# A hybrid diffusion block on one core: both token parts of a product in one 512-column matmul, each in its half of a PSUM bank, and down tiles between all up groups

## The chip, the core and the metric

The kernel runs on 1 core of one Trainium2 chip. The metric is the device time of one execution in microseconds, the lower the better. Engines are called TensorE (PE in rows; its weight loads PEld), VectorE (DVE), ScalarE (ACT), GpSimd (POOL) and SyncE (SP, which issues most loads).

## What is computed

One layer (`DEPTH = 1`) over 512 tokens of width 2048: a conditioned norm, a chunked gating MLP, a second norm, and a gated FFN with a width-3 convolution along the tokens. Only the FFN is touched by the change:

```
def conv_ffn(h, w_up, conv_w, conv_b, w_down):
    z = dwconv(h @ w_up, conv_w, conv_b, FFN_CONV // 2)
    g, v = jnp.split(z, 2, axis=-1)
    return (jax.nn.silu(g) * v) @ w_down
...
h_lat = h_lat + m_l[:, :, 5] * conv_ffn(n_l, ffn_w_up[i], ffn_conv_w[i], ffn_conv_b[i], ffn_w_down[i])
return rmsnorm(h_lat, final_g)
```

`w_up` is 2048 x 11264 (5632 gate and 5632 value columns), `w_down` 5632 x 2048.

## The kernel before

**Number format.** Every factor is split into a high part, rounded to the type that TensorE multiplies, and a low part, what is left (`split`, L71: the high one on ScalarE, L72, the low one on VectorE, L73). A product is three matmuls, `mm3` (L66): high weights x high tokens, high x low, low x high. Weights are the stationary operand and are loaded anew for each matmul.

**The FFN in chunks.** The 5632 columns are 11 chunks (`fc`) of 512. Chunk 0 runs plainly (`f0_comp`, `f1_comp`, in halves of 256 tokens). Chunks 1 to 10 save one multiplication in eight: for a pair of 128-row tiles of the tokens and a pair of 128-column tiles of the weights, the 2 x 2 x 2 products over the two token halves are replaced by **7 products** of sums and differences, each 128 x 128 weights by 256 tokens. `t_pair` (L667) makes the sums of tokens once; `s_prep` (L773) loads the weights of two pairs, forms their 4 sums on VectorE (L778 to L780) and splits both: a tile of 768 columns (plain weights) and one of 1024 (sums).

**Units.** All work is a list of units. An *up group* (`up_group`, L964) makes 256 of the gate columns (`vpart` 0) or value columns (`vpart` 1) of a chunk: 4 units, each `s_comp` with two pairs. The 7 products are summed over all 8 pairs in PSUM, two products in the halves of one bank, 4 banks. `s_evac` (L792) then forms the four results from the seven sums with one ScalarE copy and 4 VectorE additions, in the tile `z`, and `conv_evac` (L693) does the convolution, the SiLU, and for a value group the product with the gate and its split. A *down* unit (`d_comp`, L866) is 24 matmuls of 512 columns; two of them fill 4 banks, and `d_evac` (L844) scales each bank into a tile `a` (pool `part`, 3 buffers) and GpSimd adds that to `hD` in device memory by a DMA.

**What sets the order.** The loop over units (L1022) calls a unit's `comp`, then the `prep` of the unit two further on (`LOOK = 2`), and between them takes `deferred` work with `pop`. `s_evac`, `conv_evac` and `d_evac` are deferred. From there a scheduler sets each engine's queue, which then runs in order. Of the tiles, `wpool` has 4 high and 4 low buffers (an up unit takes two of each, a down unit one), `raw` 6 buffers for loads and sums, `ps` 8 PSUM banks. Per chunk the order of units is (L973): up, 4 down, up, 4 down, up, up; in the last chunk up, 2 down, up, 2 down, up, up, 4 down.

```
                for out, (sh, sl), q, mov, new in (
                        (d[:, L], (h3, l3), 0, lo(X1), True),
...
                    mm3(out, sh[:, k, q, :], sl[:, k, q, :], *mov, first and new, last, True)
```

Of the kernel before, what the change touches and what calls it, by code (L numbers as in the profile page):

```python
# [12 lines left out]
P = 128  # L13
# [23 lines left out]
def build(tc, ctx, x, xT, cvec, adaT, ada_b, norm_g, w_in, g_v, w_sT, b_s, w_out,  # L37
# [588 lines left out]
    x1, x2, x3, x4, b12 = [{} for _ in range(5)]  # L626
# [4 lines left out]
    tmade = [0]  # L631
# [5 lines left out]
    def pair_t(dst, p):  # L637
        if p not in dst:
            dst[p] = blk_t(F32R), blk_t(F32R)
        return dst[p]  # L640
# [3 lines left out]
    def n_tile(th, d):  # L644
# [3 lines left out]
        def f():  # L648
# [6 lines left out]
            if th == 0:  # L655
                h, l = pair_t(x1, p)
                split(h[:, half(j)], l[:, half(j)], t)
            elif j == 0:
                b12[p] = blk_t(F32R)
                split(b12[p][:, L], b12[p][:, R], t)  # L660
            else:
                h, l = pair_t(x2, p)
                split(h[:, L], l[:, L], t)
# [3 lines left out]
    def t_pair(p):  # L667
        def f():
# [6 lines left out]
            h, l = pair_t(x2, p)  # L675
# [38 lines left out]
    def half_tok(th, k):  # L714
        p, j = k // 2, k % 2
        if th == 0:
            return [x[:, half(j)] for x in x1[p]]
        if j == 0:
            return b12[p][:, L], b12[p][:, R]
        return [x[:, L] for x in x2[p]]  # L720

# [10 lines left out]
    def f_mm(th, k2, w):  # L732
        h, l = w
        for i in range(4):
            for a in range(2):
# [4 lines left out]
                mm3(state["fp"][i][:, half(th)], h[:, cs], l[:, cs], *half_tok(th, k),  # L740
# [19 lines left out]
    def f1_comp(k2):  # L760
        def f(w):
# [30 lines left out]
    def s_evac(cp, acc):  # L792
        a, b, c, d = acc

        def f():
            z = spat.tile([P, D], F32, tag="s", name="z")

            def at(i, n=1):
                return z[:, i * HT:(i + n) * HT]
            two = lambda x: x.rearrange("p (n t) -> p n t", n=2)  # L800
            dup = lambda x: x.unsqueeze(1).to_broadcast([P, 2, HT])
# [5 lines left out]
            state["z", cp] = z  # L807
        return f

    def s_comp(fc, i2, vpart, u):  # L810
        cp = vpart * (FF // 256) + fc * 2 + i2

        def f(w):
            (h3, l3), (h4, l4) = w
            while tmade[0] < min(2 * u + 2, NP):
                pop()
            if u == 0:
                state["sp7"] = [bank() for _ in range(4)]
            a, b, c, d = state["sp7"]
            for k in range(2):  # L820
                p = 2 * u + k
                X1, X2, X3 = x1[p], x2[p], x3[p]
                X4 = x4[p][:, L], x4[p][:, R]
                lo = lambda x: [y[:, L] for y in x]
                hi = lambda x: [y[:, R] for y in x]
                first, last = p == 0, p == NP - 1
                for out, (sh, sl), q, mov, new in (
                        (d[:, L], (h3, l3), 0, lo(X1), True),
# [37 lines left out]
    def d_comp(fc, q):  # L866
        def f(w):
# [4 lines left out]
            for i in range(4):  # L872
# [4 lines left out]
                if q % 2:  # L877
                    deferred.append(d_evac(fc, q // 2 * 4 + i, state["dp"][i]))
# [220 lines left out]
```

## Time and profile before

| | us |
|---|---|
| median of 3 runs | 2536.16 (2535.04 to 2540.63) |
| the profiled execution | 2533.04 |
| its span, first to last instruction | 2531.3 |
| TensorE busy (matmuls) | 2488.6, 98% |
| TensorE weight loads | 2223.9, 88% |
| VectorE busy | 1759.8, 70% |
| ScalarE busy | 1100.1, 43% |
| mean granted TensorE clock | 0.997 of full speed |

The busy share of TensorE counts pipelined matmuls, so it doesn't tell how near each matmul is to its shortest spacing; that is read from the starts of neighbouring matmuls. VectorE's next operation starts some 0.08 us before the end of the one ahead, so what an operation costs in a full queue is also read from start to start. The FFN's chunks 1 to 10 run from about 1195 to 2475 us.

### The profile page before, as it was taken

Reading aid. Unit: us, or ns where it says so; the run is one execution under the profiler, and the core shown is the slowest. Engines: PE = TensorE matmul, PEld = TensorE weight load, DVE = VectorE, ACT = ScalarE, POOL = GpSimd, SP = SyncE. Lnnn points to the kernel's source line nnn. Section 1 sums busy time; section 2 is a strip of 40 time slices with the busy share of each in tenths; the row PEclk is TensorE's granted clock in tenths of the full one; section 3 lists DMA queues with packets and bytes.
Section 4 is the critical chain, followed back from the end, with each engine's and each line's share of the span. In section 5 each row is a group of like instructions: output and inputs, shape, how many; then the busy total and the mean of one; then the engine's idle time right before and its main releaser. Section 6 shows DMA issues by size and latency. Waiting matters only on the chain.

```text
span 2531.3 us, 37809 instructions
## 1 busy us (share of the span) xinstructions
PE 2488.6 (98%) x14888; PEld 2223.9 (88%) x14888; DVE 1759.8 (70%) x2877; ACT 1100.1 (43%) x1595; POOL 149.4 (6%) x182
## 2 busy tenths in 40 slices
PE   7999999999999999999999999999999999999998
PEld 5888888878888888899999999999999999999998
DVE  6895577567676437469658686767677777767775
ACT  7422234333334224347445454545444444444454
POOL 0000000000000000000010101111111111111011
PEclk9999999999999999999999999999999999999999
DMA  7885555555555446524364655555555556565573
GB/s 274 293 309 188 190 185 187 171 173 186 182 187 183 157 157 210 199 90 136 94 141 135 141 133 134 139 135 140 128 147 129 148 120 157 118 150 117 142 193 107
DMA packets 166042, 411.69 MB, mean 163 GB/s; under 512 B 15460, under 2 KB 25828, under 8 KB 165864
## 3 DMA queue, kind: packets, MB, share of 16 engines
q1 hardware_dynamic: 139432, 361.04, 44.5%
q0 software_dynamic: 24320, 46.15, 11.5%
q8 instruction: 116, 1.90, 0.3%
q10 hardware_dynamic: 2112, 2.10, 0.2%
q14 instruction: 62, 0.51, 0.1%
HBM read 358.89 MB, written 50.33 MB: 162 GB/s over the span
## 4 chain that ended last, share of the span: by engine, by line
PE 83%; DMA 7%; DVE 7%; issue 2%; ACT 1%; SPq 0%; DVEq 0%; ACTq 0%
PE p L62 83%; DMA r<-in_adaT 6%; DVE r L131 2%; DVE wl L73 2%; DMA r<-in_w_in 1%; ACT wh L72 1%; DVE b L367 0%; DVE b L73 0%; DVE b L468 0%; DVE sp L450 0%; DVE b L471 0%; DVE b L362 0%; DVE r L930 0%; ACT b L270 0%; ACT b L72 0%
## 5 line engine op out<-in xcount | busy, mean ns | idle before, releaser
L62 PE MATMUL p<-b,wh 128*128 128x256 f32 (+1 forms) x8256 | 1905.4, 325 | 0.1
L62 PEld LDWEIGHTS p<-b,wh 128*128 128x128 f32 x8256 | 1388.9, 190 | 126.2 <-ACT wh L72 0.3
L62 PE MATMUL p<-b,wl 128*128 128x256 f32 (+1 forms) x4128 | 1340.0, 325 | 2.9 <-DVE wl L73 2.8
L72 ACT ACTIVATE wh<-r 128x1024 fp32r<-128x1024 f32 (+2 forms) x457 | 438.2, 969 | 970.2 <-PE p L62 792.3
L62 PEld LDWEIGHTS p<-b,wl 128*128 128x128 f32 x4128 | 784.6, 190 | 68.0 <-DVE wl L73 3.7
L73 DVE TENSOR_TENSOR wl<-r,wh 128x1024 fp32r<-128x1024 f32 (+2 forms) x457 | 505.0, 1110 | 207.7 <-ACT wh L72 207.0
L131 DVE SCALAR_TENSOR_TENSOR r<-r,cb 128x1024 f32<-128x1024 f32 x192 | 233.4, 1222 | 263.3 <-DMA r<-in_adaT 262.4
L62 PE MATMUL p<-wh,b 128*128 128x512 f32 x992 | 310.4, 391 | 0.8 <-ACT wh L72 0.8
L848 POOL DMA_DIRECT2D hD<-a x160 | 139.7, 907 | 2294.8 <-ACT a L847 2293.8
L73 DVE TENSOR_TENSOR wl<-s,wh 128x1024 fp32r<-128x1024 f32 x160 | 195.6, 1222 | 106.6 <-ACT wh L72 106.6
L62 PEld LDWEIGHTS p<-wh,b 128*128 128x128 f32 x992 | 186.2, 188 | 40.0 <-ACT wh L72 1.9
L62 PE MATMUL p<-wl,b 128*128 128x512 f32 x496 | 193.8, 391 | 3.1 <-DVE wl L73 3.1
L778 DVE TENSOR_TENSOR s<-r 128x512 f32<-128x512 f32 x160 | 110.0, 688 | 100.5 <-DMA r<-in_w_up 99.5
L72 ACT ACTIVATE wh<-s 128x1024 fp32r<-128x1024 f32 x160 | 167.6, 1048 | 19.5 <-PE p L62 19.4
L847 ACT ACTIVATE a<-p,m 128x512 f32<-128x512 f32 x160 | 109.0, 686 | 127.6 <-DMA hD<-a 79.8
L62 PEld LDWEIGHTS p<-wl,b 128*128 128x128 f32 x496 | 93.2, 188 | 24.4 <-DVE wl L73 5.6
L62 PE MATMUL p<-b 128*128 128x256 f32 (+1 forms) x624 | 85.0, 297 | 5.3 <-ACT b L72 5.3
L62 PEld LDWEIGHTS p<-b 128*128 128x128 f32 x624 | 79.5, 194 | 9.1 <-ACT b L72 6.6
L780 DVE TENSOR_TENSOR s<-s,r 128x256 f32<-128x256 f32 x160 | 67.7, 423 | 3.8
L779 DVE TENSOR_TENSOR s<-s,r 128x256 f32<-128x256 f32 x160 | 67.6, 422 | 3.8
L73 DVE TENSOR_TENSOR b<-b 128x512 fp32r<-128x512 f32 (+3 forms) x117 | 62.4, 561 | 5.2 <-ACT b L72 4.8
L72 ACT ACTIVATE b<-b 128x512 fp32r<-128x512 f32 (+3 forms) x117 | 55.8, 518 | 1.3 <-DVE b L672 1.1
(109 smaller groups left out, 1150.7 us busy)
## 6 DMA issues: line engine op xcount, KB each, us to landing
r<-in_adaT SPq DMA_DIRECT2D x192, 512.0 KB, 4.5
r<-in_w_up SPq DMA_DIRECT2D x184, 512.0 KB, 3.7
r<-in_w_in SPq DMA_DIRECT2D x121, 512.0 KB, 4.1
r<-in_w_down SPq DMA_DIRECT2D x88, 512.0 KB, 4.9
hD<-a POOLq DMA_DIRECT2D x160, 256.0 KB, 5.2
r<-in_w_out SPq DMA_DIRECT2D x64, 512.0 KB, 4.7
b<-in_x SPq DMA_DIRECT2D x16, 256.0 KB, 5.4
b<-in_xT SPq DMA_DIRECT2D x16, 256.0 KB, 6.5
```

The source lines that it names most:

```text
L62: nc.tensor.matmul(out, lhsT, rhs, start=first, stop=last, skip_group_check=shared)
L72: nc.scalar.activation(hi, src, AF.Copy)
L73: nc.vector.tensor_sub(lo, src, hi.bitcast(F32))
L131: nc.vector.scalar_tensor_tensor(r[b], r[b], 1.0, state["cb"][b], op0=ALU.mult, op1=ALU.mult, accum_out=m2[:, b, j:j + 1])
L778: nc.vector.tensor_add(s[:, :, 0:2, :], r[:, :, 0:1, :].to_broadcast([P, 2, 2, P]), r[:, :, 1:4:2, :])
L779: nc.vector.tensor_add(s[:, :, 2, :], s[:, :, 1, :], r[:, :, 1, :])
L780: nc.vector.tensor_add(s[:, :, 3, :], s[:, :, 2, :], r[:, :, 2, :])
L847: nc.scalar.activation(t, p, AF.Copy, scale=m[:, 5 * ND + d:5 * ND + d + 1])
L848: nc.gpsimd.dma_start(out=hD[d * P:(d + 1) * P, :], in_=t, accum_op=ALU.add)
```

## The change

Each operand of tokens is now one tile, `tok[name, pair]`, with its high part in the left 256 columns and its low part in the right ones (`tok_split`; the names are B11 to B22, N1, N2, T3, T4). A product is `mm3w`: the high weights times the whole tile, 512 columns, and the low weights times the left half, 256 columns. The sum of a product therefore fills a whole bank, high part left and low part right, and an up group has 7 banks. `s_evac` adds the two halves as well. It and `d_evac` are called at once and not deferred; `conv_evac` stays deferred, and `s_evac` first takes all that read the one `z` tile (`zlive`). Behind the first value chunk (`f1_comp`) the four banks are copied to `z`, and the convolution reads them there. Two down units stand behind each up group; in the last chunk behind the first two groups, and four at the end, as before.

```diff
+    def mm3w(bank, sh, sl, w, first, last):
+        n = w.shape[-1] // 2
+        mm(bank, sh, w, first, False, True)
+        mm(bank[:, :n], sl, w[:, :n], False, last, True)
...
+    def tok_split(name, p, src):
+        t = tok[name, p] = blk_t(F32R)
+        split(t[:, L], t[:, R], src)
...
-            h, l = pair_t(x2, p)
-            split(h[:, R], l[:, R], e[:, R])
-            split(*pair_t(x3, p), t)
-            x4[p] = blk_t(F32R)
-            split(x4[p][:, L], x4[p][:, R], o[:, R])
+            tok_split("N1", p, e[:, R])
+            tok_split("N2", p, o[:, R])
+            tok_split("T3", p, t[:, L])
+            tok_split("T4", p, t[:, R])
...
-                    deferred.append(conv_evac(0, i, 1, state["fp"][i]))
+                    nc.scalar.activation(z[:, i * T:(i + 1) * T], state["fp"][i], AF.Copy)
+                    conv_later(0, i, 1, z[:, i * T:(i + 1) * T])
...
-            nc.scalar.activation(at(3), d[:, L], AF.Copy)
-            nc.vector.tensor_add(two(z)[:, :, L], dup(at(3)), two(c))
-            nc.vector.tensor_add(two(at(5, 2)), dup(at(4)), two(a))
-            nc.vector.tensor_add(at(1, 2), at(5, 2), b)
-            nc.vector.tensor_add(at(3), at(6), a[:, L])
...
+    SEVEN = ((0, 0, "B11"), (1, 1, "N1"), (0, 1, "B21"), (1, 2, "N2"), (1, 0, "T3"),
+             (1, 3, "B22"), (0, 2, "T4"))
...
+        while zlive[0]:
+            pop()
+        z = spat.tile([P, D], F32, tag="s", name="z")
+        b1, b5, b2, b6, b7, b3, b4 = acc
...
+        def plus(o, i, b):
+            add(at(o), at(i), b[:, L])
+            add(at(o), at(o), b[:, R])
+        for o, b in ((4, b1), (5, b5)):
+            nc.scalar.activation(at(o), b[:, R], AF.Copy)
+            add(at(o), at(o), b[:, L])
+        plus(0, 4, b2)
+        plus(6, 4, b6)
+        plus(7, 6, b7)
+        z4 = z.rearrange("p (n s t) -> p n s t", n=4, s=2)
+        add(z4[:, 0:2, 1, :], z[:, 6 * HT:].rearrange("p (n t) -> p n t", n=2),
+            at(5).unsqueeze(1).to_broadcast([P, 2, HT]))
+        plus(1, 1, b3)
+        plus(2, 7, b4)
...
+            for b, (g, q, name) in zip(state["sp7"], SEVEN):
+                sh, sl = w[g]
+                for k in range(2):
+                    p = 2 * u + k
+                    mm3w(b, sh[:, k, q, :], sl[:, k, q, :], tok[name, p], p == 0, p == NP - 1)
...
-                    deferred.append(d_evac(fc, q // 2 * 4 + i, state["dp"][i]))
+                    d_evac(fc, q // 2 * 4 + i, state["dp"][i])
...
     for fc in range(1, NFC):
         last = fc == NFC - 1
-        up_group(fc, 0, 0)
-        down(fc - 1, range(0, 2 if last else 4))
-        up_group(fc, 0, 1)
...
+        for j, (i2, vpart) in enumerate(((0, 0), (0, 1), (1, 0), (1, 1))):
+            up_group(fc, i2, vpart)
+            if not last or j < 2:
+                down(fc - 1, range(2 * j, 2 * j + 2))
```

How the queues change is shown at three places of an up group in the middle of the program. Lines of the changed kernel are some 7 above those of before in its first part (`split` is L79 and L80 there). In the rows `wh` and `wl` are high and low parts of weights, `p` a PSUM bank, `s` a tile of sums of weights, `r` a load, `b` a tile of tokens or of the gated result, `a` a scaled down tile.

**TensorE, the first two products of a unit (`s_comp`), before:**

```order
L62 MATMUL p_19585<-b_8817,wh_19634 128x256 [waits Activation_49]
L62 MATMUL p_19585<-b_8818,wh_19634 128x256
L62 MATMUL p_19585<-b_8817,wl_19635 128x256 [waits DVE_49]
...
L62 MATMUL p_19584<-b_8817,wh_19634 128x256
L62 MATMUL p_19584<-b_8818,wh_19634 128x256
L62 MATMUL p_19584<-b_8817,wl_19635 128x256
```

and now, the second unit of the group behind a value group:

```order
L62 MATMUL p_16323<-b_8774,wh_16315 128x512
L62 MATMUL p_16323<-b_8774,wl_16316 128x256 [waits DVE_49]
L62 MATMUL p_16323<-b_8805,wh_16315 128x512
L62 MATMUL p_16323<-b_8805,wl_16316 128x256
L62 MATMUL p_16324<-b_9345,wh_16319 128x512 [waits Activation_49]
L62 MATMUL p_16324<-b_9345,wl_16320 128x256 [waits DVE_49]
```

A product is two matmuls for three, and both pairs of a product follow each other; the second product is the first that takes the sums of weights (`wh_16319`, `wl_16320`).

**ScalarE behind the additions of a value group that is followed by down, before** (L698 is the convolution's first step, L847 the four `d_evac`, L72 with `b` the split of the gated tile, with `wh` the high part of weights):

```order
L698 ACTIVATE t_19834<-z_19800,cw_407 128x512 [waits DVE_49]
L698 ACTIVATE t_19849<-z_19800,cw_407 128x512 [waits DVE_49]
L72 ACTIVATE wh_19931<-r_19925 128x768 [waits DMAHW5_49,PE_49,Activation_49]
L72 ACTIVATE b_19839<-t_19834 128x512 [waits DVE_49]
L847 ACTIVATE a_19882<-p_19806,m_95 128x512 [waits DMASW5_49,PE_49]
L847 ACTIVATE a_19891<-p_19807,m_95 128x512 [waits DMASW6_49,PE_49]
L72 ACTIVATE b_19854<-t_19849 128x512 [waits DVE_49]
L847 ACTIVATE a_19922<-p_19808,m_95 128x512 [waits DMASW7_49,PE_49]
L72 ACTIVATE wh_19935<-s_19927 128x1024 [waits PE_49,Activation_49]
L847 ACTIVATE a_19939<-p_19809,m_95 128x512 [waits DMASW0_49,PE_49,Activation_49]
```

and now (`wh_16319` is the one of the TensorE rows above):

```order
L695 ACTIVATE t_16213<-z_16191,cw_407 128x512 [waits DVE_49]
L695 ACTIVATE t_16250<-z_16191,cw_407 128x512
L845 ACTIVATE a_16279<-p_16222,m_95 128x512 [waits DMASW1_49,PE_49]
L845 ACTIVATE a_16288<-p_16223,m_95 128x512 [waits DMASW2_49,PE_49]
L845 ACTIVATE a_16297<-p_16224,m_95 128x512 [waits DMASW3_49,PE_49]
L79 ACTIVATE b_16218<-t_16213 128x512 [waits DVE_49]
L845 ACTIVATE a_16306<-p_16225,m_95 128x512 [waits DMASW4_49,PE_49,Activation_49]
L79 ACTIVATE b_16255<-t_16250 128x512 [waits DVE_49]
L79 ACTIVATE wh_16319<-s_16311 128x1024
```

The fourth `d_evac` has moved ahead of the second split of the gated tile and of the 1024-wide high part.

**VectorE, the additions of a value group, before** (L803 to L806):

```order
L803 TENSOR_TENSOR z_19800<-z_19800,p_19584 128x2x256 [waits PE_49,Activation_49]
L804 TENSOR_TENSOR z_19800<-z_19800,p_19582 128x512 [waits DVE_49,PE_49]
L805 TENSOR_TENSOR z_19800<-z_19800,p_19583 128x512 [waits DVE_49,PE_49]
L806 TENSOR_TENSOR z_19800<-z_19800,p_19582 128x256
L73 TENSOR_TENSOR wl_19846<-r_19843,wh_19845 128x1024 [waits DMAHW3_49,Activation_49]
```

and now, with the subtraction ahead of them (`wl_16160`, down's weights) and the first 9 of 13:

```order
L771 TENSOR_TENSOR s_16311<-r_16309 128x2x256 [waits DMAHW2_49,DVE_49]
L772 TENSOR_TENSOR s_16311<-s_16311,r_16309 128x2x128 [waits DVE_49]
L80 TENSOR_TENSOR wl_16160<-r_16157,wh_16159 128x1024 [waits DMAHW7_49,PE_49,Activation_49]
L814 TENSOR_TENSOR z_16191<-z_16191,p_16038 128x256 [waits Activation_49]
...
L80 TENSOR_TENSOR wl_16210<-r_16207,wh_16209 128x1024 [waits DMAHW0_49]
L810 TENSOR_TENSOR z_16191<-z_16191,p_16042 128x256 [waits DVE_49,PE_49]
L80 TENSOR_TENSOR wl_16266<-r_16259,wh_16265 128x768 [waits PE_49,Activation_49]
L811 TENSOR_TENSOR z_16191<-z_16191,p_16042 128x256 [waits DVE_49]
L80 TENSOR_TENSOR wl_16270<-s_16261,wh_16269 128x1024 [waits PE_49,Activation_49]
L819 TENSOR_TENSOR z_16191<-z_16191 128x2x256 [waits DVE_49]
```

and further on in the same queue, up to the low part that the second unit needs:

```order
L704 TENSOR_TENSOR t_16250<-t_16250,b_15969 128x512 [waits DVE_49]
L772 TENSOR_TENSOR s_16360<-s_16360,r_16358 128x2x128
L80 TENSOR_TENSOR b_16219<-t_16213,b_16218 128x512 [waits Activation_49]
L773 TENSOR_TENSOR s_16360<-s_16360,r_16358 128x2x128 [waits DVE_49]
L80 TENSOR_TENSOR b_16256<-t_16250,b_16255 128x512 [waits Activation_49]
L771 TENSOR_TENSOR s_16402<-r_16400 128x2x256 [waits DMAHW4_49]
L80 TENSOR_TENSOR wl_16320<-s_16311,wh_16319 128x1024 [waits PE_49,Activation_49]
```

The additions now stand behind an add that waits for a load, three subtractions of weights stand among them, and `wl_16320` stands behind the second split's low half.

## Rows read from the trace of the kernel before

**Rows 1.** The chain that ended last, in order of time: start, us, engine, releaser.

```profile
1180.66 1336.09 PE p L62 x9420
```

**Rows 2.** Stretches of 50 us: busy time and count of PE, PEld, DVE, ACT, POOL.

```profile
1150.00:1200.00 50.00, 46.97 (x383) 45.95 (x383) 49.19 (x95) 35.48 (x62) 0.00 (x0) 1.00 0.43 135
...
1450.00:1500.00 50.00, 50.00 (x397) 49.04 (x396) 46.93 (x68) 25.10 (x33) 0.00 (x0) 1.00 0.41 127
```

**Rows 3.** PE in order of time (start, us, line): up to down, then down to up.

```profile
1990.75 0.28 PE L62 MATMUL p<-b,wl 128*128 128x256 f32 x1
...
1991.11 0.28 PE L62 MATMUL p<-b,wl 128*128 128x256 f32 x1
1991.23 0.63 PE L62 MATMUL p<-b,wh 128*128 128x512 f32 x2
...
1999.87 0.39 PE L62 MATMUL p<-b,wl 128*128 128x512 f32 x1
...
2012.79 0.39 PE L62 MATMUL p<-b,wl 128*128 128x512 f32 x1
2013.02 0.40 PE L62 MATMUL p<-b,wh 128*128 128x256 f32 x2
```

**Rows 4.** Groups by line and shape: count, busy us and mean ns, idle before.

```profile
L803 DVE TENSOR_TENSOR z<-z,p 128x512 f32<-128x512 f32 x40 | 27.2, 680 | 0.6 <-ACT z L802 0.5
```

**Rows 5.** DVE in order of time, 1936 to 1988 us: start, us, line.

```profile
1936.39 0.96 DVE L73 TENSOR_TENSOR wl<-r,wh 128x768 fp32r<-128x768 f32 x1 [1.69 <-ACT wh L72]
...
1940.95 0.69 DVE L778 TENSOR_TENSOR s<-r 128x512 f32<-128x512 f32 x1 [2.39 <-DMA r<-in_w_up]
1941.68 0.43 DVE L779 TENSOR_TENSOR s<-s,r 128x256 f32<-128x256 f32 x1
...
1974.68 0.41 DVE L806 TENSOR_TENSOR z<-z,p 128x256 f32<-128x256 f32 x1
1975.01 0.42 DVE L779 TENSOR_TENSOR s<-s,r 128x256 f32<-128x256 f32 x1
1975.46 0.43 DVE L780 TENSOR_TENSOR s<-s,r 128x256 f32<-128x256 f32 x1
...
1977.13 0.95 DVE L73 TENSOR_TENSOR wl<-r,wh 128x768 fp32r<-128x768 f32 x1
1978.04 1.23 DVE L73 TENSOR_TENSOR wl<-s,wh 128x1024 fp32r<-128x1024 f32 x1
1979.18 1.41 DVE L701 SCALAR_TENSOR_TENSOR t<-z,cw,t 128x511 f32<-128x511 f32 x2
...
1981.80 0.96 DVE L73 TENSOR_TENSOR wl<-r,wh 128x768 fp32r<-128x768 f32 x1
1982.67 0.68 DVE L73 TENSOR_TENSOR b<-t,b 128x512 fp32r<-128x512 f32 x1
1983.28 1.22 DVE L73 TENSOR_TENSOR wl<-s,wh 128x1024 fp32r<-128x1024 f32 x1
...
1987.28 0.69 DVE L778 TENSOR_TENSOR s<-r 128x512 f32<-128x512 f32 x1 [2.18 <-DMA r<-in_w_up]
```

**Rows 6.** Who waited for whom: us in total, times, longest us.

```profile
DVE s L778 <- DMA r<-in_w_up: 99.5, 49, 5.1
```

**Rows 7.** ACT in order of time, around 1955 us.

```profile
1955.18 1.52 ACT L698 ACTIVATE b<-z,cw 128x512 f32<-128x512 f32 x2 [2.76 <-DVE z L805]
```

**Rows 8.** The `d_evac` line on ACT in order of time, and its DMA's time to landing.

```profile
1760.79 0.69 ACT L847 ACTIVATE a<-p,m 128x512 f32<-128x512 f32 x1 [0.79 <-PE p L62]
...
1767.03 0.69 ACT L847 ACTIVATE a<-p,m 128x512 f32<-128x512 f32 x1 [1.38 <-DMA hD<-a]
...
2411.85 0.69 ACT L847 ACTIVATE a<-p,m 128x512 f32<-128x512 f32 x1 [3.86 <-DMA hD<-a]
2412.43 0.84 ACT L72 ACTIVATE wh<-r 128x768 fp32r<-128x768 f32 x1
...
DMA to landing us min/median/max: 3.9/5.2/8.1
```

**Rows 9.** Groups by line and shape: the high half of the gated tile's split.

```profile
L72 ACT ACTIVATE b<-t 128x512 fp32r<-128x512 f32 x67 | 41.9, 626 | 17.4 <-DVE t L707 14.3 <-DVE t L674 2.5
```

More of the change, by code (lines that the diff above doesn't have):

```diff
@@ L625, in build @@
     NP = ND // 2
-    x1, x2, x3, x4, b12 = [{} for _ in range(5)]
+    tok = {}
     hD = dram.tile([D, T], F32, name="hD")
@@ L654, in f @@
             nc.scalar.activation(t, t, AF.Identity, bias=m[:, c:c + 1], scale=A[:, 1, d:d + 1])
[L655 to L661, printed above, removed]
-                h, l = pair_t(x2, p)
-                split(h[:, L], l[:, L], t)
+            tok_split("B%d%d" % (j + 1, th + 1), p, t)
             made[th] += 1
@@ L738, in f_mm @@
                 cs = slice(b * P, (b + 1) * P)
-                mm3(state["fp"][i][:, half(th)], h[:, cs], l[:, cs], *half_tok(th, k),
+                t = tok["B%d%d" % (k % 2 + 1, th + 1), k // 2]
+                mm3(state["fp"][i][:, half(th)], h[:, cs], l[:, cs], t[:, L], t[:, R],
                     k == 0 and th == 0, k == ND - 1, True)
@@ L817, in f @@
             if u == 0:
[L818 to L828, printed above, removed]
-                        (c[:, L], (h3, l3), 1, hi(X1), True),
-                        (c[:, R], (h4, l4), 2, X4, False),
-                        (a[:, L], (h4, l4), 1, hi(X2), True),
-                        (a[:, R], (h4, l4), 0, lo(X3), False),
-                        (b[:, L], (h4, l4), 3, lo(X2), True),
-                        (b[:, R], (h3, l3), 2, hi(X3), False)):
-                    mm3(out, sh[:, k, q, :], sl[:, k, q, :], *mov, first and new, last, True)
+                state["sp7"] = [bank() for _ in SEVEN]
@@ L841, in s_comp @@
         return f
     def d_evac(fc, d, p):
-        def f():
-            t = part.tile([P, T], F32, tag="a", name="a")
-            nc.scalar.activation(t, p, AF.Copy, scale=m[:, 5 * ND + d:5 * ND + d + 1])
-            nc.gpsimd.dma_start(out=hD[d * P:(d + 1) * P, :], in_=t, accum_op=ALU.add)
-            if fc == NFC - 2:
-                ht[d] = blk_t()
-                nc.gpsimd.dma_start(out=ht[d], in_=hD[d * P:(d + 1) * P, :])
-        return f
+        t = part.tile([P, T], F32, tag="a", name="a")
@@ L854, in d_load @@
+        nc.scalar.activation(t, p, AF.Copy, scale=m[:, 5 * ND + d:5 * ND + d + 1])
+        nc.gpsimd.dma_start(out=hD[d * P:(d + 1) * P, :], in_=t, accum_op=ALU.add)
+        if fc == NFC - 2:
+            ht[d] = blk_t()
+            nc.gpsimd.dma_start(out=ht[d], in_=hD[d * P:(d + 1) * P, :])
     def d_load(fc, q):
@@ L971, in down, with twice @@
             units.append((d_prep(fc, q), d_comp(fc, q), after and after(q)))
+    def twice(q):
+        a, b = e_prep(2 * (q - 4)), e_prep(2 * (q - 4) + 1)
+        return lambda: (a(), b())
     for fc in range(1, NFC):
         last = fc == NFC - 1
-        up_group(fc, 0, 0)
-        down(fc - 1, range(0, 2 if last else 4))
-        up_group(fc, 0, 1)
+        for j, (i2, vpart) in enumerate(((0, 0), (0, 1), (1, 0), (1, 1))):
+            up_group(fc, i2, vpart)
+            if not last or j < 2:
+                down(fc - 1, range(2 * j, 2 * j + 2))
         if last:
-            down(fc - 1, range(2, 4))
-        else:
-            down(fc - 1, range(4, 8))
-        up_group(fc, 1, 0)
-        up_group(fc, 1, 1)
-        if last:
-            def twice(q):
-                a, b = e_prep(2 * (q - 4)), e_prep(2 * (q - 4) + 1)
-                return lambda: (a(), b())
             down(fc - 1, range(4, 8), twice)
```

41 lines of the change are left out of this document (14 added, 27 removed).

## Prediction

> **What bounds the kernel now.** I read the chain of waits first. From 1180.66 us on it is one entry: 1336 us of TensorE and nothing else [rows 1]. The reader is to see that in nearly the whole gated FFN, the part that is changed, no other engine and no transfer holds TensorE up, so only shorter TensorE work, or a new wait of TensorE, can move the time there. Second, the stretches: TensorE is busy for 50 of 50 us from 1450 to 1500, with VectorE at 47 [rows 2]. That is where three up groups follow each other, and VectorE is nearly full there already. Third, TensorE's starts [rows 3]. In a run of 512-column matmuls 57 starts take 12.92 us, 0.2267 us each; in a run of 256-column ones three take 0.36, 0.120 each. Twice the 256 spacing is 0.240, so a matmul costs 0.0133 us that its columns don't explain. The spacing belongs to the matmul that goes first: a 512 is followed by a 256 after 0.23, a 256 by a 512 after 0.12. So a product made of one 512 and one 256 should take 0.2267 + 0.120 = 0.3467, against 3 x 0.120 = 0.360 now.
>
> **The gain.** There are 40 up groups of 8 pairs of tiles with 7 products: 2240 products, each with one matmul and one weight load less. 2240 x 0.0133 = 29.9 us. The columns stay the same. Up groups fall from 20.16 to 19.41 us, all of it on the path.
>
> A rule of the Trainium skill speaks against this: TensorE: Matmul & The Clock Gate, section Back-to-back issue gap, gives columns/2.4 GHz plus 2.5 ns for each matmul at the full clock. By it the term would be 2240 x 2.5 ns = 5.6 us; the trace disagrees, with 120 ns and 227 ns where it has 109 and 216.
>
> **What is added.** Each up group ends in 13 additions for 4 and one more ScalarE copy. A 512-wide add took 0.68, a 256-wide one 0.41 [rows 4, 5], so VectorE gets 12 x 0.41 + 0.69 - (3 x 0.68 + 0.41) = 3.2 us more per group. With two down units behind most groups a group's turn is 19.4 + 48 x 0.2267 = 30.3 us of TensorE, against VectorE's, start to start: per unit three adds and two subtractions, 0.73 + 0.45 + 0.33 + 0.91 + 1.14 = 3.56, four times 14.2; down 2 x 1.14 = 2.3; additions 12 x 0.33 + 0.60 = 4.6; the convolution's four steps 2 x 1.41 = 2.8 [rows 5]. That is 23.9 for a gate group, and 26.3 for a value group, which has two products and two low halves of 0.60 more. So on average VectorE fits. What counts is who waits in which queue.
>
> Banks: a group takes 7 of 8 and down 4, so each reuse waits for an evacuation. Worked through, all hold: the first sums of the seven are read while the last products still run, and the down banks that the next group's last products need are evacuated some 3 us before. I cost this at nothing; the cover is gone if the additions start over 3 us late.
>
> The queue that does not hold is ScalarE's after a **value** group. Set 0 at the end of its last matmul. The two down units run to 10.88, then the next group's units of 4.85: the second starts at 15.73. Its sixth matmul is the first that takes the 1024-wide low part (the sums of weights), behind a product of 0.69 and a 512: 15.73 + 0.69 + 0.23 = **16.65**. In the new order the 1024-wide high part stands in ScalarE's queue behind the fourth `d_evac` and the second split of the gated tile; before it stood ahead of the fourth `d_evac`, and the split ahead of both. The fourth `d_evac` waits for the DMA of the first, since `part` has 3 buffers. Step by step:
> - When the additions start: two weight loads in series set it. A load can go when the 768-wide low part of two units before has freed its buffer; from that subtraction's start to the add that waits for the load took 4.56 and, at worst here, 5.48 [rows 5], with 49 such waits in all [rows 6]. I take 4.7. The first subtraction is at 16.5 of the group before (tiles free at 15.7, ScalarE's copy), so 16.5 + 4.7 + 0.6 (the add) + 4.7 = 26.5, then two adds and the low part of down, 0.73 + 0.45 + 1.14: 28.8, which is 1.5 before this group's end.
> - The additions with the three weight subtractions that the order puts among them, start to start: 12 x 0.33 + 0.60 + 2 x 1.14 + 0.91 = 7.8 [rows 5]. They end at 6.3.
> - Two conv copies on ScalarE, 1.5 [rows 7], stand ahead of the first `d_evac`: it starts at 7.8, not at 7.0 when its bank is done.
> - From the first to the fourth `d_evac`: 6.24, the middle one of 23 sets that ran at TensorE's pace [rows 8]. 14.0. The transfer takes 3.9 to 8.1, median 5.2 [rows 8], so this step lies between 4.9 and 9.1.
> - Behind it: 0.58 to the next ScalarE start, 0.63 for the split, then on VectorE its low half 0.60, an add that stands in between 0.60, and the subtraction 1.22 [rows 5, 8, 9]: 3.65. **17.7**.
> TensorE waits 1.0 us. This comes behind every value group that is followed by down and another up group: 2 in each of nine chunks and 1 in the last, 19. **19 x 1.0 = 19 us.** Bounds: nothing if both DMA steps are at their fast end (first to fourth 5.5, loads 4.5: the end is 16.6); 2.0 us each, 38 in all, if their means are 6.7 and 4.95. I take the value from the middle rows. Behind a gate group the 1024-wide copy stands ahead of the fourth `d_evac` and the low part ends near 14.5: no wait.
>
> Smaller terms. The eight `t_pair` calls split four 256-wide halves for two halves and a 512: by 4 x 0.41 - (2 x 0.41 + 0.68) = 0.14 us each on VectorE, in a stretch where TensorE already lost 3 of 50 us and VectorE had 49 [rows 2]: **+1 us**, bounds 0 and 2. In the last chunk no down stands between the third and the fourth group: from the end of the second TensorE has 10.9 + 38.8 = 49.7 us, VectorE 8 x 3.56 + 2 x 4.6 + 2 x 2.8 + 2.4 + 2.3 = 48. That is too near full for no wait: **+2**, bounds 0 and 5. The four ScalarE copies behind the first value chunk free banks that are needed 2.8 us later: nothing. `d_evac` called at once, not deferred: no work more, the order above is its price.
>
> Sum against the profiled execution of 2533.04 us (a span of 2531.3): -29.9 + 19 + 1 + 2 = -7.9, so 2525.1. That execution is 3.1 under the median of 2536.16; at the median **2528.3**.
>
> **Rivals.**
> - *No wait behind the value groups.* The order is the same but the transfers come back sooner, or additions start earlier. For it: the wait is 1 us at the end of a sum of some 18, and the down evacuations are spread more evenly than now. Against: the row of the middle transfer, and that several were longer. 2536.2 - 29.9 + 3 = **2509**. 27 in 100.
> - *Slower: the same queue, a longer wait.* Place: the second unit behind a value group, where ScalarE stands at the fourth `d_evac`. It decides from 27 us in all, 1.4 us a group: then the gain is gone. The steps add: a later start of the additions delays the first `d_evac`, and the fourth follows it. With 5.1 for the loads and 6.7 for the evacuations it is 17.7 + 0.8 + 0.5 = 19.0, a wait of 2.3, or 44 us: **2553**. For it: loads of 5.48 and transfers up to 8.1 are there. Against: most were near the middle. 19 in 100.
> - *The removed matmul gives nothing back*, because the columns are the same. If the 0.0133 belonged to the columns and not to the matmul, the waits alone would be left: 2536.2 + 22 = **2558**. Against it stands that two 256 spacings are more than one of 512, and that the spacing changes with the first matmul of each pair [rows 3]. 4 in 100. By the page's rule above it would be this rival less 5.6 us.
>
> **How the numbers follow.** My forecast has 50 in 100, with a wait of 0.6 to 1.6 us: 2520 to 2540, 2528.3 in the middle. 0.2% of the median is 5.1 us, about what a measurement of this kernel can tell from no change: faster is below 2531.1, slower above 2541.2. Faster: the first rival's 27 and 29 of the forecast's 50, together 0.56. Same: the forecast's other 21 and 1 of the second rival, 0.22. Slower: 18 and 4, 0.22. The range reaches down over the first rival to 2507 and up into the second to 2547, which leaves out some 4 below and 16 above.
>
> **What would show it.** TensorE's up groups with 14 starts in 4.85 us, 0.2267 and 0.120 in turn. In the waits, TensorE on `wl` of the subtraction or `wh` of the copy, 19 times about 1 us, each behind a fourth `d_evac` that waited for `hD`. VectorE some 128 us busier (40 x 3.2). I am wrong if TensorE waits for banks (its releaser is then an addition or a `d_evac`), if the spacing of a 512 before a 256 is above 0.23, or if the waits stand behind gate groups too.

## The result, and the profile after

The changed kernel takes 2573.03 us (median of 4 runs, 2567.93 to 2580.62), the kernel before 2536.73 beside it: a ratio of 1.0151, 95% interval 1.0136 to 1.0165. It is slower by 36 us; I had forecast 8 us faster, and the range ended at 2547. The profiled execution took 2569.19 us with a span of 2567.4, 36.1 more than the span before. By stages, from the starts of TensorE's matmuls:

| | before | after | us | forecast |
|---|---|---|---|---|
| up to the second norm's first column sum | 1117.02 | 1109.27 | -7.8 | 0 |
| from there to the first up group | 108.9 | 115.4 | +6.6 | +1 |
| chunks 1 to 10, to the last 512-column matmul | 1242.2 | 1279.9 | +37.7 | -8.9 |
| the rest of the matmuls | 52.2 | 52.2 | 0 | 0 |

(The first up group before starts at 1225.87: its first down matmul at 1246.03 less 56 products of 0.36.) The loss is in chunks 1 to 10. The starts of their 2240 products split it: those that follow each other without a stall take 0.3516 us instead of 0.360, 18.8 us less in all, and 72 products take longer, by 54.2 us together. 44.3 us of these stand in the second unit behind the 19 value groups that a down pair and another up group follow, 2.3 each; 9.0 in the last units of the value groups themselves.

The stretches of 50 us of the changed kernel that answer to [rows 2], and one more (us, then busy time of PE, PEld, DVE, ACT, POOL; last the granted clock, DMA share and GB/s):

```profile
1150.00:1200.00 50.00, 42.75 (x329) 41.65 (x328) 43.82 (x91) 28.93 (x54) 0.00 (x0) 0.93 0.34 109
1450.00:1500.00 50.00, 48.56 (x258) 40.95 (x257) 35.65 (x61) 23.39 (x31) 4.40 (x5) 1.00 0.54 134
...
1850.00:1900.00 50.00, 48.42 (x237) 40.66 (x237) 42.65 (x75) 22.73 (x31) 6.17 (x7) 0.97 0.49 124
```

TensorE, never idle there before in the stretch from 1450, now is by 1.4 us in 50; VectorE, 46.93 there before, has 35.65: on average the stage isn't short of VectorE. What TensorE waits for stands in its own row order; this is the changed kernel's TensorE in the second unit behind a value group that ended at 1594.88 (in brackets the idle time before, and what ended it):

```profile
1610.38 0.40 PE L62 MATMUL p<-b,wh 128*128 128x512 f32 x1
1610.61 0.28 PE L62 MATMUL p<-b,wl 128*128 128x256 f32 x1
1610.73 0.40 PE L62 MATMUL p<-b,wh 128*128 128x512 f32 x1
...
1611.33 0.28 PE L62 MATMUL p<-b,wl 128*128 128x256 f32 x1
1612.51 0.50 PE L62 MATMUL p<-b,wh 128*128 128x512 f32 x1 [0.91 <-ACT wh L79]
1614.03 0.39 PE L62 MATMUL p<-b,wl 128*128 128x256 f32 x1 [1.02 <-DVE wl L80]
```

It stalls twice, for the 1024-wide high part and then for its low part. Upstream of it, ScalarE of the changed kernel:

```profile
1602.54 1.53 ACT L695 ACTIVATE t<-z,cw 128x512 f32<-128x512 f32 x2 [1.36 <-DVE z L811]
1603.97 1.82 ACT L845 ACTIVATE a<-p,m 128x512 f32<-128x512 f32 x3
1607.59 0.63 ACT L79 ACTIVATE b<-t 128x512 fp32r<-128x512 f32 x1 [1.80 <-DVE t L704]
1610.31 0.69 ACT L845 ACTIVATE a<-p,m 128x512 f32<-128x512 f32 x1 [2.08 <-PE p L62]
1610.90 0.62 ACT L79 ACTIVATE b<-t 128x512 fp32r<-128x512 f32 x1
1611.42 1.04 ACT L79 ACTIVATE wh<-s 128x1024 fp32r<-128x1024 f32 x1
```

This is the queue of the forecast [rows 8]: three `d_evac`, a split, 2.08 us of standing at the fourth (the bank that the row names was long done; it is the transfer of the first), the second split, the high part. Ahead of that VectorE, from the 768-wide low part of the value group's third unit to the additions (L814 is the first) and to the late low part:

```profile
1580.56 0.96 DVE L80 TENSOR_TENSOR wl<-r,wh 128x768 fp32r<-128x768 f32 x1 [1.38 <-ACT wh L79]
1581.51 1.23 DVE L80 TENSOR_TENSOR wl<-s,wh 128x1024 fp32r<-128x1024 f32 x1
1587.75 0.69 DVE L771 TENSOR_TENSOR s<-r 128x512 f32<-128x512 f32 x1 [5.02 <-DMA r<-in_w_up]
1588.36 0.95 DVE L80 TENSOR_TENSOR wl<-r,wh 128x768 fp32r<-128x768 f32 x1
1589.23 0.42 DVE L772 TENSOR_TENSOR s<-s,r 128x256 f32<-128x256 f32 x1
1589.56 1.22 DVE L80 TENSOR_TENSOR wl<-s,wh 128x1024 fp32r<-128x1024 f32 x1
...
1592.50 0.69 DVE L771 TENSOR_TENSOR s<-r 128x512 f32<-128x512 f32 x1 [1.38 <-DMA r<-in_w_up]
...
1593.57 1.22 DVE L80 TENSOR_TENSOR wl<-r,wh 128x1024 fp32r<-128x1024 f32 x1
1594.70 0.74 DVE L814 TENSOR_TENSOR z<-z,p 128x256 f32<-128x256 f32 x2
...
1612.76 1.22 DVE L80 TENSOR_TENSOR wl<-s,wh 128x1024 fp32r<-128x1024 f32 x1
```

For 5.02 us VectorE stands at a sum for the **next** group's first unit, whose load hasn't landed. Behind it, in order, stand the low parts of this group's last unit (1588.36 and 1589.56), and TensorE has to wait for the second of them:

```profile
1590.84 0.39 PE L62 MATMUL p<-b,wl 128*128 128x256 f32 x1 [0.48 <-DVE wl L80]
```

The load itself (the queue of SP, its one load in 1581 to 1582, time to landing):

```profile
L124 SPq DMA_DIRECT2D r<-in_w_up x1: 341/341/341, 1581.5 to 1581.5; - x1
...
DMA to landing us min/median/max: 6.1/6.1/6.1
```

It took 6.1 us; the fastest loads near there took 3.1. Four additions to `hD` were issued from 1573.8 to 1580.2 and landed after 5.2 to 6.3, so the last two were still on their way. So it is at all 19 places: one addition (4 times) or two (15 times) were under way when this load was issued, and it took 4.2 to 8.2 us, 5.9 in the middle. The changed kernel's waits that answer to [rows 6] and others (us, times, longest):

```profile
DVE s L771 <- DMA r<-in_w_up: 213.6, 75, 7.1
...
ACT a L845 <- DMA hD<-a: 53.8, 33, 3.2
...
PEld p L62 <- DVE wl L80: 46.5, 45, 5.7
```

VectorE's wait for loads is the one that doubled, from 99.5 us in 49 times; ScalarE's for `hD` became shorter (79.8 before).

### The profile page after: what moved, and what is told of

Its sections match the earlier page's. It is cut to its first block, busy times and chain, and to the rows that moved or that the text cites. A ratio compares the mean times of both kernels' runs of the same rounds, so it can differ in the third digit from the quotient of the medians.

```text
span 2567.4 us, 33870 instructions
## 1 busy us (share of the span) xinstructions
PE 2490.6 (97%) x12648; PEld 2110.0 (82%) x12648; DVE 1837.5 (72%) x3245; ACT 1098.9 (43%) x1647; POOL 150.5 (6%) x182
## 5 line engine op out<-in xcount | busy, mean ns | idle before, releaser
L62 PE MATMUL p<-b,wh 128*128 128x512 f32 (+1 forms) x6016 | 1897.5, 385 | 12.8 <-ACT wh L79 12.5
L62 PEld LDWEIGHTS p<-b,wh 128*128 128x128 f32 x6016 | 1112.5, 189 | 242.6 <-ACT wh L79 17.6
L79 ACT ACTIVATE wh<-r 128x1024 fp32r<-128x1024 f32 (+2 forms) x457 | 438.8, 970 | 1162.8 <-PE p L62 1079.4
L80 DVE TENSOR_TENSOR wl<-r,wh 128x1024 fp32r<-128x1024 f32 (+2 forms) x457 | 506.8, 1110 | 146.6 <-ACT wh L79 142.1
L771 DVE TENSOR_TENSOR s<-r 128x512 f32<-128x512 f32 x160 | 110.2, 689 | 213.7 <-DMA r<-in_w_up 213.6
L80 DVE TENSOR_TENSOR wl<-s,wh 128x1024 fp32r<-128x1024 f32 x160 | 195.3, 1221 | 10.4 <-ACT wh L79 8.9
L79 ACT ACTIVATE wh<-s 128x1024 fp32r<-128x1024 f32 x160 | 167.2, 1045 | 6.7 <-PE p L62 4.9
L845 ACT ACTIVATE a<-p,m 128x512 f32<-128x512 f32 x160 | 103.8, 677 | 73.7 <-DMA hD<-a 53.8
L62 PEld LDWEIGHTS p<-b 128*128 128x128 f32 x624 | 79.8, 195 | 9.1 <-ACT b L79 6.6
L80 DVE TENSOR_TENSOR b<-t,b 128x512 fp32r<-128x512 f32 (+1 forms) x75 | 46.8, 633 | 43.7 <-ACT b L79 43.6
L810 DVE TENSOR_TENSOR z<-z,p 128x256 f32<-128x256 f32 x200 | 76.3, 415 | 0.3 <-PE p L62 0.2
L811 DVE TENSOR_TENSOR z<-z,p 128x256 f32<-128x256 f32 x200 | 76.3, 415 | 0.0
L773 DVE TENSOR_TENSOR s<-s,r 128x256 f32<-128x256 f32 x160 | 67.4, 421 | 1.6
```

Source lines behind the costliest of these rows:

```text
L62: nc.tensor.matmul(out, lhsT, rhs, start=first, stop=last, skip_group_check=shared)
L79: nc.scalar.activation(hi, src, AF.Copy)
L80: nc.vector.tensor_sub(lo, src, hi.bitcast(F32))
L771: nc.vector.tensor_add(s[:, :, 0:2, :], r[:, :, 0:1, :].to_broadcast([P, 2, 2, P]), r[:, :, 1:4:2, :])
L773: nc.vector.tensor_add(s[:, :, 3, :], s[:, :, 2, :], r[:, :, 2, :])
L810: add(at(o), at(i), b[:, L])
```

## Experiments

"Theory A" and so on are named in the texts that were written ahead of the runs. Ratios are to the kernel before, run on the same chip.

**Buffers alone (three kernels).** The first has 4 buffers `a`; the second 8 load buffers (`raw`) and 66 tiles in `blk`; the third 4 buffers `a`, 7 load buffers and 67 tiles. The edit of the first:

```diff
-    blk = ctx.enter_context(tc.tile_pool(name="blk", bufs=70))
-    part = ctx.enter_context(tc.tile_pool(name="part", bufs=3))
+    blk = ctx.enter_context(tc.tile_pool(name="blk", bufs=69))
+    part = ctx.enter_context(tc.tile_pool(name="part", bufs=4))
```

> The changed kernel with 4 buffers `a` instead of 3 (and 69 block tiles instead of 70). Changed kernel: 2573, before: 2536.7. Theory A, late loads start the chain and the buffer only passes it on: the fourth d_evac starts without waiting for hD, so the 19 stalls in the second unit behind the value groups (44 us together) go, but VectorE still stands some 200 us at L771 for loads and the 9 us in the last units of the value groups stay: 2527 to 2532. Theory B, the buffer is the only cause: the same 44 us go and L771 is no matter: 2527 to 2532 too, the two part in the next run. Theory C, VectorE has too much to do and its queue is late whatever is waited for: at most half of the 44 us goes, 2551 or more.

> The changed kernel with 8 load buffers instead of 6 (and 66 block tiles instead of 70), so the load for the next group's first unit can go a unit earlier; `a` has 3 buffers. Theory A: L771's waits for loads fall from 214 us to under 50, the additions start at least 1.5 us earlier, the fourth d_evac still waits for hD but early enough: the 44 us go to under 10 and the 9 us in the last units of value groups go too: 2520 to 2530. Theory B: L771's waits fall, but the fourth d_evac follows its bank's time and hD, and the 44 us stay to more than half: 2550 to 2570. Theory C: 2555 to 2573.

> 4 buffers `a` and 7 load buffers (67 block tiles). All theories but C: no stall of over 5 us in sum is left in chunks 1 to 10 and the shorter products (0.3516 us against 0.360, 2240 of them: 19 us) show whole: 2516 to 2524. Theory C: above 2540.

They took 2562.55 (ratio 1.0114, 1.0098 to 1.0131), 2592.77 (1.0231, 1.0216 to 1.0247) and 2575.07 (1.0163, 1.0141 to 1.0184). By the time alone the first and the third lie where theory C had them (2551 or more, above 2540), the second above every range. But what holds TensorE up is in none of the texts. In the first, TensorE waits for weights no more, but it waits in a place that was quiet before; TensorE of the first in its order of time, the down pair behind one group of each chunk:

```profile
1337.18 0.39 PE L62 MATMUL p<-b,wl 128*128 128x512 f32 x1
1338.35 0.74 PE L62 MATMUL p<-b,wh 128*128 128x512 f32 x2 [0.78 <-ACT a L845]
...
1342.18 0.74 PE L62 MATMUL p<-b,wh 128*128 128x512 f32 x2 [0.78 <-ACT a L845]
```

The scheduler orders by its own notion of the time, and with other buffers it orders otherwise: here it finishes the four down banks one after the other, and each waits for the evacuation of the one ahead: 36 waits in each of the three kernels, 35, 33 and 29 us. The second and the third have 27 and 17 us of stalls in products besides. The buffers and the order changed at once, so these runs settle nothing, but that stalls behind value groups can go (none left in the first). The next runs on buffers keep the order.

**Smaller transfers to `hD`.** Sixteen of 512 columns are added and the rest of each addition is left out; the queues come out as in the changed kernel.

```diff
-        nc.gpsimd.dma_start(out=hD[d * P:(d + 1) * P, :], in_=t, accum_op=ALU.add)
+        nc.gpsimd.dma_start(out=hD[d * P:(d + 1) * P, 0:16], in_=t[:, 0:16], accum_op=ALU.add)
```

> The changed kernel, but only 16 of the 512 columns of each down result are added to hD; the rest of the addition is left out. Buffers as in the changed kernel. Theory A with the transfers to hD as the reason why loads are late: a load takes 3.3 us where it took 5 to 7, L771's waits fall from 214 us to under 110, the fourth d_evac hardly waits: 2515 to 2526. Theory A with the load buffers alone as the reason (a load goes late, but lands as fast as ever): L771's waits stay over 170, yet the small transfer lands in under 3 us, so most of the 44 us go: 2528 to 2540. Theory B: as that, 2528 to 2540. Theory C: above 2550.

2517.85, ratio 0.9941 (0.992 to 0.9963). Not one product stalls, and chunks 1 to 10 take 1228.2 us: the whole 54 us come from the transfers to `hD`. VectorE has the same work as in the changed kernel, so theory C is out. The 1228.2 us also show what the shorter products are worth undisturbed: 1242.2 - 1228.2 = 14 us. Its waits for loads, and the load that answers to the one of 6.1 us (of 18 such loads the middle one took 3.3):

```profile
DVE s L771 <- DMA r<-in_w_up: 161.4, 75, 4.1
...
L124 SPq DMA_DIRECT2D r<-in_w_up x1: 340/340/340, 1569.8 to 1569.8; - x1
...
DMA to landing us min/median/max: 3.3/3.3/3.3
```

Less than 213.6, the longest 4.1 instead of 7.1, but not under 110 as I had put it: VectorE still stands at loads, only not long enough to hold TensorE up. In the gate groups these loads took 4.0 us or more here too; why stays open.

**Four buffers `a`, queues held.** Here, in the pairs of 512 and in the last four kernels every engine's queue in chunks 1 to 10 is chained to the changed kernel's order, but for the moves that are named; in the two kernels on the order of units it is not. Three small constant tiles make the room (two of them now lie in tiles of `blk`), so that `blk` stays at 70. No run holds the queues and changes nothing else.

```diff
-    part = ctx.enter_context(tc.tile_pool(name="part", bufs=3))
+    part = ctx.enter_context(tc.tile_pool(name="part", bufs=4))
...
+    for names in ORDER["lists"]:
+        chain = [traced[at[n]] for n in names if mark[0] <= at[n] < mark[1]]
+        for a, b in zip(chain, chain[1:]):
+            tc.add_manual_dep(b, a.name, mybir.DependencyInfo(
+                mybir.DependencyClass.NoSync, mybir.DependencyReason.DATA), reason="order as before")
```

> 4 buffers `a` instead of 3 and nothing else moved: every engine's queue of chunks 1 to 10 is held to the order of the changed kernel, and room for the fourth buffer comes from three small constant tiles, so there are 70 block tiles and 6 load buffers as before. Changed kernel 2573, before 2536.7. Theory B (the fourth d_evac's wait for hD, with its 3 buffers, is the root of all: behind value groups it holds up the high part of the sums of weights, behind gate groups the 768-wide high part, whose low part then frees a load buffer late): all 54 us of stalls go: 2518 to 2524. Theory A (the transfers to hD make loads slow, and VectorE is late by that): the 44 us in the second units go, the 9 us in the last units of value groups stay, L771 still waits some 200 us: 2527 to 2532.

2533.8, ratio 0.9997 (0.9986 to 1.0008). The 44 us in the second units fell to 4.6, and 10.5 us in the last units of the value groups stayed. VectorE's waits for loads there (L776 is L771):

```profile
DVE s L776 <- DMA r<-in_w_up: 232.3, 75, 7.3
```

That is theory A: the buffer takes the end of the chain away, and its beginning, the late load, is as it was. The time is 2 us over theory A's range. In its profiled execution (2539.11 us) the first up group starts at 1230.34, in the changed kernel's at 1224.71, so those 5.6 us lie ahead of the chunks, which take 1244.2 us.

**Pairs of 512.** The same, with the matmuls of a product's two pairs ordered by width.

```diff
-                for k in range(2):
-                    mm3w(b, sh[:, k, q, :], sl[:, k, q, :], tok[name, p + k], p + k == 0, p + k == NP - 1)
+                for k in range(2):
+                    mm(b, sh[:, k, q, :], tok[name, p + k], p + k == 0, False, True)
+                for k in range(2):
+                    mm(b[:, L], sl[:, k, q, :], tok[name, p + k][:, L], False, p + k == NP - 1, True)
```

> As the pinned kernel with 4 buffers, but the two pairs' matmuls of a product run as 512, 512, 256, 256 columns instead of 512, 256, 512, 256. In the changed kernel a 512 followed by a 256 took 0.235 us and a 256 followed by a 512 took 0.117; in runs of one width they took 0.2267 and 0.120. If the cost sits where a 512 is followed by a 256, two products take 0.2267 + 0.235 + 0.120 + 0.117 = 0.699 instead of 0.703: 1120 times 0.0046, 5 us faster than the pinned kernel. If every matmul carries the same cost whatever follows, no difference (within 3 us).

2531.9, ratio 0.9993 (0.9981 to 1.0005). The time alone can't be told from no difference. By the starts the products take 0.348 us each instead of 0.352, 9 us in all, nearly twice what I had put down; the stalls grew from 16.9 to some 22 and took half of it. That every matmul carries the same cost is out by that; that the cost sits only where a 512 is followed by a 256 is not borne out either: in the pairs that step takes 0.233, the one from a 512 to the other 0.233 too and not 0.2267, and the two steps behind a 256 take 0.115 and 0.116.

**The order of units alone**, in the kernel before, with its 4 banks and 256-column matmuls:

```diff
-        up_group(fc, 0, 0)
-        down(fc - 1, range(0, 2 if last else 4))
...
+        for j, (i2, vpart) in enumerate(((0, 0), (0, 1), (1, 0), (1, 1))):
+            up_group(fc, i2, vpart)
+            if not last or j < 2:
+                down(fc - 1, range(2 * j, 2 * j + 2))
```

> The kernel before with three 256-column matmuls to a product and 4 banks, and only the order of units of the change: two down units behind every up group. If the order of units alone brings the stalls (four d_evacs of one down pair in each turn, 3 buffers `a`): 20 us or more of TensorE waits, 2550 or more. If it takes the 12 more additions and the evacuation at once as well: under 5 us of waits, 2532 to 2541.

2598.09, ratio 1.025 (1.0235 to 1.0266): the order of units, with the queues that the scheduler makes of it, costs 63.5 us by itself, with no matmul and no addition changed, as the first half of the expectation had it. Its waits (ScalarE at `d_evac` 79.8 us before, VectorE at loads 99.5, TensorE at low parts 5.9):

```profile
DVE s L778 <- DMA r<-in_w_up: 234.2, 104, 6.8
ACT a L847 <- DMA hD<-a: 157.4, 41, 5.5
...
PE p L62 <- DVE wl L73: 46.8, 78, 3.7
```

**The matmuls and additions alone**, with the order of units before (the loop of the last diff put back, TensorE held to the order as written):

> The changed kernel's matmuls, banks and additions with the order of units before: up, 4 down, up, 4 down, up, up; TensorE is held to the order as written. If the new order of units is what hurts: 2518 to 2528. If three up groups in a row are too much for VectorE (some 14.2 for the weights, 4.6 for the additions and 2.8 for the convolution against 19.7 us of TensorE to a group, 2 to 4 us too long, 20 groups): TensorE waits 30 us or more for low parts and for banks, 2550 or more.

2547.36, ratio 1.0048 (1.0033 to 1.0063). Stalls of 35 us in the products, in the three groups that follow each other; among them TensorE now waits for banks, which the additions free:

```profile
PEld p L62 <- DVE wl L80: 32.8, 36, 5.7
...
PE p L62 <- DVE z L811: 12.0, 10, 1.8
```

So the second half of the expectation holds in kind, 3 us short of its 2550: three groups in a row are too much with the 13 additions. The two parts of the change depend on each other, and neither alone is faster.

**The sums behind the low parts.** The changed kernel's queues with 3 buffers `a`, but the sums of weights of the next group's first two units moved on VectorE behind the low parts of two units ahead, 74 places:

> The changed kernel with 3 buffers `a`, its queues held as they are, but for one thing: on VectorE the three sums of weights for the next group's first two units (they wait for a load) stand behind the low parts that are needed sooner (those of this group's last unit and of the first down unit) and no longer ahead of them; 74 places. Theory D, VectorE standing at that load is what makes the additions late: the additions start some 1.7 us sooner, so the stalls behind value groups fall from 2.3 us to about 0.6 each (44 to some 12) and the 9 us in the last units of value groups go: 2573 - 41 = 2532, 2526 to 2540. Theory B, the buffer `a` alone sets the wait behind value groups: only the 9 us go: 2560 to 2566.

2528.13, ratio 0.9964 (0.9952 to 0.9975): of the 36 us lost, all came back and 8 more, as theory D had it (theory B: 2560 or more). VectorE behind its value group (which ended at 1582.63; L776 to L778 are the sums, L819 the first addition):

```profile
1573.94 1.23 DVE L85 TENSOR_TENSOR wl<-s,wh 128x1024 fp32r<-128x1024 f32 x1
1575.08 0.69 DVE L776 TENSOR_TENSOR s<-r 128x512 f32<-128x512 f32 x1
...
1580.82 0.74 DVE L819 TENSOR_TENSOR z<-z,p 128x256 f32<-128x256 f32 x2
...
1598.58 1.22 DVE L85 TENSOR_TENSOR wl<-s,wh 128x1024 fp32r<-128x1024 f32 x1
```

The sum no longer waits: its load has landed by the time it comes up. In the whole program VectorE's waits there fell from 213.6 us to this:

```profile
DVE s L776 <- DMA r<-in_w_up: 5.9, 7, 1.6
```

The additions start 1.8 us before the group's end, where it was 0.2; the stalls of the second units are 9.5 us in 18 places, 0.5 each; the last units of the value groups have none. The fourth `d_evac` still waits for `hD` (41 times, 71.3 us), early enough.

**Both cures, and with pairs.**

> 4 buffers `a` and the sums of weights behind the low parts. The kernel with 4 buffers alone took 2533.8, with 17 us of stalls left in the products, nearly all for low parts. Theory D: under 4 us of stalls are left: 2517 to 2524. If the stalls that are left come from the transfers to hD that slow the loads, wherever VectorE waits for them: L771's wait moves to another place and 10 us or more stay: 2528 to 2535.

> As the one ahead, with the two pairs' matmuls of a product as 512, 512, 256, 256. There two products took 0.6956 us against 0.7046, 1120 times 0.009 = 10 us less, which 5 us of longer stalls and the spread of runs hid. With the stalls gone: 2507 to 2516. If low parts are now late again because TensorE reaches them sooner: as the one ahead, 2517 to 2526.

2518.82, ratio 0.9929 (0.9909 to 0.9949), and 2508.51, ratio 0.9887 (0.987 to 0.9904). In both no product stalls (0.35 us once in the second). The first has the 1228.2 us of the small transfers: with these two places mended, `hD` costs nothing. Both times lie where the cures were to be enough (2517 to 2524, 2507 to 2516). The second is the fastest version here, 1.1% under the kernel before. Its TensorE, two 512 and two 256 in turn:

```profile
1384.96 0.63 PE L67 MATMUL p<-b,wh 128*128 128x512 f32 x2
1385.42 0.40 PE L67 MATMUL p<-b,wl 128*128 128x256 f32 x2
1385.65 0.63 PE L67 MATMUL p<-b,wh 128*128 128x512 f32 x2
```

**The first chunk.** The last one, with four low parts of the plain chunk 15 places earlier on VectorE:

> As the kernel with 4 buffers, the sums behind the low parts and the matmuls in pairs (ratio 0.9887 to the kernel before), and in the plain first chunk four low parts of weights stand 15 places earlier on VectorE, ahead of pieces of the token sums (t_pair) that nothing needs so soon. There TensorE waited 7.8 us at four low parts, and the stage took 92.0 us instead of 85.4 before the change. If the wait is a matter of the queue's order: the waits there sum to under 2 us and 6 to 8 us go, ratio 0.9855 to 0.9865 (2500 to 2503 beside 2536). If VectorE simply has too much to do in that stage (busy 49 of 50 us there before the change): TensorE waits at later low parts instead, the same 7 us in sum, ratio 0.988 to 0.990.

2510.33, ratio 0.9899 (0.9882 to 0.9915): no gain. The stage from the second norm to the first up group took 119.6 us, 115.4 in the kernel ahead. TensorE's waits there became 11.7 us from 7.8, the longest now for a high part:

```profile
1162.30 0.39 PE L68 MATMUL p<-b,wl 128*128 128x256 f32 x1 [2.69 <-DVE wl L86]
...
1172.91 2.08 PE L68 MATMUL p<-b,wh 128*128 128x256 f32 x8 [7.47 <-ACT wh L85]
```

Neither half of the expectation had this: the high part that TensorE waited for (ScalarE, 1171.82) stood in ScalarE's queue behind a split that had waited 1.71 us for a piece of `t_pair` on VectorE. What would cure this stage stays open.

## Why the prediction was wrong

Point by point, by its steps:

- **The gain.** 29.9 us were forecast, 18.8 came by the products' starts, and the stage as a whole took 14 less where nothing stalled. The columns and the count were right; the spacing was mis-sized. I took a 512 in a run of 512s (0.2267) and a 256 in a run of 256s (0.120) [rows 3]. Where they alternate, a 512 is followed after 0.235 and a 256 after 0.117: 0.3516, 5 ns more on each product, 11 us in all. The ends of long runs in the kernel before didn't show it (21 of each): there a 512 goes to a 256 after 0.2266 and a 256 to a 512 after 0.120, as inside the runs. I took those ends for the alternation. In pairs 0.348 was reached, near the 0.3467 of the forecast. The Trainium skill's page TensorE: Matmul & The Clock Gate, section Back-to-back issue gap, gives a fixed 2.5 ns for an isolated matmul, which would have made the term 5.6 us, an estimate by that page. The measured 18.8 lies between it and mine.
- **The queue behind value groups.** Place, count (19) and order were right. Against the forecast, counted from the group's end (1594.88 in the rows above): the additions with their subtractions took 7.84 us (7.8), the conv copies 1.43 (1.5), from the first `d_evac` to the fourth 6.34 (6.24), from there to the end of the low part 3.67 (3.65). Every one of these steps held. The end came at 19.1, not at 17.7, since the additions started 0.2 us before the end and not 1.5. The stall is 19.1 - 16.65 = 2.45, where I had 1.0.
- **The step that failed: "two weight loads in series ... I take 4.7."** From the 768-wide low part to the sum that waits for the load took 7.19 and 4.14 in the rows above, 11.3 where I had 9.4. Over the 19 value groups the additions start 0.5 us before the end in the mean; in the three where they start 1.9 or more before it, the stall is 0.2 to 0.7 us. I had the price from [rows 5], with the down units of the kernel before, four behind each of two groups in four. In the new order one or two additions to `hD` were under way each time the next group's first load was issued, and it took 5.9 us in the middle; with the small transfers it took 3.3. That the load is slow by `hD` is shown by the small transfers (longest wait 4.1 instead of 7.1). That the sum standing at this load makes the additions late is shown by the sums moved behind the low parts: with 3 buffers the additions then start 1.8 before the end, the fourth `d_evac` comes at 13.5 (forecast 14.0), and the low part ends at 17.2 (17.7), with 0.5 us of a stall. The evacuation is the other link: with a fourth buffer the stalls behind value groups fall to 4.6 us although the loads are as late. The Trainium skill's page DMA: Bandwidth & Descriptors, section Queues, rings and completion order, says that each DMA engine takes the queues that have work in turn. The trace is in line with it, 5.9 us beside `hD` and 3.3 beside the small transfers; the turns themselves no run shows. I had not asked what the moved transfers would meet.
- **"Behind a gate group ... no wait"** held for the low part that I meant (0.1 us there), and failed by the same step in another place. Behind a gate group the late load holds VectorE in the last unit of the value group that follows, and the low parts behind it in the queue come late: 9.0 us in 14 places. I had asked only who waits for the additions, not what else stands behind the waiting sum.
- **The rivals.** The slower one, the same queue with a wait of 2.3 us, 44 in all, is what happened; I gave it 19 in 100, and put its time at 2553, 20 us too low: its gain was 11 too large, and the 9 us in the last units weren't in it. That its 44 came out to the microsecond is partly luck: 5.5 of the 44.3 are products at a lower clock (last section), which I had not forecast. Of the signs of being wrong that I had set, two came: a spacing of a 512 before a 256 above 0.23, and waits that follow from a gate group too, those in the last units.
- **t_pair**: +1 was forecast, the stage took 6.6 us more. TensorE waited 5.48 us for a low part that stood behind pieces of several `t_pair` calls, and the granted clock of 1150 to 1200 is 0.93, where it was 1.00 [rows 2]. I costed VectorE's work, not the queue.
- **The last chunk**: +2 was forecast, 0.2 came. **Banks: nothing** held in the changed kernel; TensorE waited for a bank for 0.15 us once.
- VectorE is 77.7 us busier, not 128: neighbouring additions overlap, and I had counted each in full (one by one they take 226.5 us where 98.5 stood, 128 more).
- **Not explained:** the 7.8 us up to the second norm, where the queues have the same order in both kernels. The other kernels with the changed FFN are there at 1107 to 1115, the kernel before with the new order of units at 1117.11, each in one profiled execution. The difference builds up between 115 and 564 us, ahead of all that the change touches. No run here tells why.

## What to carry to other kernels

Before a group of evacuations is moved, write down which loads are issued while their transfers run, and price those loads from a stretch where the two meet. And for each wait of an in-order engine ask what stands behind the waiting instruction: here a sum for the next group was queued ahead of low parts that this group needed, and moving it behind them was worth some 45 us with no buffer added. Where a scheduler sets the order, hold the queues before a buffer is judged, or the order changes with it.

## What the chip showed that I had not expected

- A matmul's spacing depends on the widths around it, and not on the next one alone. In long runs a 512 takes 0.2267 us and a 256 0.120; where they alternate, 0.235 and 0.117. But at the end of a run of 512s, a 512 goes to a 256 after 0.2264 (38 times in the changed kernel).
- Short stalls can cost more than themselves. After stalls of 0.56 and 1.02 us TensorE ran five products at 0.64 us each instead of 0.352. The granted clock there is 0.50, which is 1.2 of 2.4 GHz, the lower of its two levels. It came behind 4 of the 19 value groups (four or five products each), 5.5 us together, which are in the 44; behind others with longer stalls it did not come (1.14 and 1.02 us at 1741, the clock 1.00 from 1739 to 1744). The changed kernel's TensorE there:

```profile
1871.48 0.39 PE L62 MATMUL p<-b,wl 128*128 128x256 f32 x1 [1.02 <-DVE wl L80]
...
1872.09 0.63 PE L62 MATMUL p<-b,wh 128*128 128x512 f32 x1
1872.51 0.41 PE L62 MATMUL p<-b,wl 128*128 128x256 f32 x1
1872.72 0.63 PE L62 MATMUL p<-b,wh 128*128 128x512 f32 x1
```

and the stretch from 1872 to 1875, its granted clock third from the end:

```profile
1872.00:1875.00 3.00, 3.00 (x11) 2.59 (x10) 2.22 (x3) 0.00 (x0) 0.00 (x0) 0.50 0.75 188
```
